# HGRN2 heads taken in pairs on tiles twice as wide, signed differences, a four-part output projection and another stream order in a two-layer hybrid trunk

## The chip, the core and the metric

The kernel runs on one core of a Trainium2 chip. The metric is device time in microseconds (us) of one execution. TensorE is called PE (PEld for its weight loads), VectorE DVE, ScalarE ACT, GpSimd POOL, and SyncE SP, whose queue issues the weight transfers.

## What is computed

A trunk of two layers on 256 tokens of 2048 features, all in float32. The change lies in layer 0, whose mixer joins two recurrences:

```python
q, f, i, g = split_cols(p_hg, HG_COLS)              # 8 heads of 128
k = (1.0 - lb) * jax.nn.sigmoid(-f)
q = jax.nn.silu(q)
o_hg = hgrn2_chunked(q, k, i, log_f)                # scores: q k exp(bcum[t] - bcum[s]), s <= t
o_hg = head_rmsnorm(unchunk_seq(o_hg), HG_HEADS, hg_norm) * jax.nn.sigmoid(g)
...
o_rw = rwkv7_scan(rh, decay, kh, vh, kk, a)         # 16 heads of 64
...
return jnp.concatenate([o_hg, o_rw], axis=-1) @ w_out
```

After each mixer comes a SwiGLU feed-forward of width 5632; layer 1 has an mLSTM and a Mamba2 mixer.

## The kernel before, in words

Every large product splits its float32 operands into a high and a low part: ACT rounds the weight tile `raw` into `whi`, DVE subtracts it into `wlo` (lines 262 and 263, seen at L262 and L109), and PE forms three products. A weight tile covers two blocks of 128 input rows; `raw`, `whi` and `wlo` have three buffers each, so ACT and DVE can be at most three tiles ahead of PE.

In layer 0 these products, the **bulk**, run beside two **lanes**, `rw` (RWKV7, four tasks of four heads, `rwkv_quad`, whose tiles are called `lane`) and `hg` (HGRN2, tiles with names that begin with h). All are Python generators that `flow` (lines 337 to 365) interleaves at build time: in each round both lanes take one step (a step that yields 1 rests one round), then the bulk takes three steps. The engines then run their own instructions in the order that is built; a list scheduler moves instructions of an engine a little within it. When the bulk reaches `wait` for a task that isn't done, it spends empty steps until the lane gets there.

The string `ORDER` sets the bulk: `p` is one pair of RWKV heads (`p0` to `p7`, products of 128x256, a task for every second one), `h` the next HGRN2 block: values and gates of four heads (`V0`, `V1`, products of 128x512), then queries and keys of two heads (`K0` to `K3`, 128x256). After `K` the HGRN2 work of its two heads is queued: a gates step `hgrn_gates` (Abs, Exp, Ln: two sets of activation tables), then `hgrn_head` for each. A head has a scan, the product qk, and for m = 1, 2, ..., 64 a function `decayed(m)`: difference, Abs, Exp, two products on DVE, then two matmuls and a copy_predicated into `hown`.

The output projection `out_proj` follows in three parts, called here Rw0 (512 rows, RWKV tasks 0 and 1), H (1024 rows, all of HGRN2) and Rw1 (512 rows, RWKV tasks 2 and 3); each ends a column block with two additions into the residual, and before Rw1 the bulk waits for RWKV task 3. The feed-forward begins behind Rw1.

Of the kernel before, what the change touches and what calls it, by code (L numbers as in the profile page):

```python
# [31 lines left out]


AHEAD = 2
ORDER = 'hhpphpphhpphpp'

EVEN_RATIO = 3.0
ODD_RATIO = 3.0
# [41 lines left out]
class Trunk:  # L80
    def __init__(self, ctx, tc, a, out):
        self.ctx, self.tc, self.nc, self.a, self.out = ctx, tc, tc.nc, a, out
        self.n = 0
        ep = lambda *x, **k: ctx.enter_context(tc.tile_pool(*x, **k))
        self.const = Arena(self.t(ep(name="const", bufs=1), [P, 1088], "const"))
# [59 lines left out]

    def masks(self):
        nc, c = self.nc, self.const
        self.rst2 = self.t(c, [P, 2, P], "rst2")
# [767 lines left out]
    def hgrn_head(self, hd, q, k, lf, vv, sg):
        nc, c, T = self.nc, self.c, self.T
        T2 = lambda tag: T(tag, (P, 2, P))
        ps2 = lambda: self.bank()[:, 0:S].rearrange("p (a t) -> p a t", t=P)
# [19 lines left out]
        own = T2("hown")  # L939
        ps = self.bank()[:, 0:8].rearrange("p (a n) -> p a n", n=4)  # L940
        for t in range(2):
            self.mm(ps[:, t, :], qk[:, t * P:(t + 1) * P], self.ones[:, 0:4])
        for t in range(2):
            self.ts(own[:, t, :], self.ident, ps[:, t, 0:1], ALU.mult)
        yield
        for m in (1, 2, 4, 8, 16, 32, 64):
            nh = P // (2 * m)
            ps = self.bank()[:, 0:P].rearrange("p (a j r) -> p a j r", a=2, r=m)
            for t in range(2):
                half = e.rearrange("p (j r) -> p j r", r=2 * m)[:, t * nh:(t + 1) * nh, m:2 * m]  # L950
                self.mm(ps[:, t], e[:, t * P:(t + 1) * P], half)
            mask = self.lev[m].bitcast(U32).rearrange("p (j r) -> p j r", r=2 * m)[:, :, m:2 * m]
            nc.vector.copy_predicated(out=own.rearrange("p a (j r) -> p a j r", r=2 * m)[:, :, :, m:2 * m],
                                      mask=mask.unsqueeze(1).broadcast_to([P, 2, nh, m]), data=ps)
            if m < 64:
                e = decayed(2 * m)
            else:

                e = T("he", bufs=3)
                self.ts(e[:, 0:P], b[:, 0:P], b[:, P - 1:P], ALU.subtract)  # L960
                self.act(e[:, 0:P], e[:, 0:P], AF.Exp, scale=-1.0)
                self.act(e[:, P:S], b[:, P:S], AF.Exp)
                self.mul(e[:, 0:P], e[:, 0:P], k[:, 0:P])
                self.mul(e[:, P:S], e[:, P:S], q[:, P:S])
# [6 lines left out]
        po = ps2()
        self.mm(po[:, 0, :], own[:, 0, :], vv[:, 0, :])
        self.mm(po[:, 1, :], cross, vv[:, 0, :], stop=False)
        self.mm(po[:, 1, :], own[:, 1, :], vv[:, 1, :], start=False)
        ss = T("hss", (P, 2))
        on = T2("hon")
        for t in range(2):
# [5 lines left out]
        for t in range(2):
            self.ts(on[:, t, :], on[:, t, :], ss[:, t:t + 1], ALU.mult)
        yield
        ps = self.bank()[:, 0:S]
        for t in range(2):
            self.tr(ps[:, t * P:(t + 1) * P], on[:, t, :])
        self.act(sg, ps.rearrange("p (t s) -> p t s", s=P), AF.Identity, scale=c["hg_norm"][:, hd:hd + 1])

# [29 lines left out]
    def gates(self, xt, bc, wk, rowp, cols):  # L1020
# [321 lines left out]
```

## Time and profile before

| | us |
|---|---|
| median of three runs | 2498.75 (2492.96 to 2506.86) |
| the profiled execution | 2492.96 |
| its span, first to last instruction | 2491.2 |
| PE busy in the span | 2446.7 |
| DVE busy | 1463.4 |
| ACT busy | 1137.6 |

The profiled execution is the fastest of the three runs; 1.8 us of it lie outside the span. In the time line, p0 begins at 124.82 us, Rw0 at 503.88, H at 535.90, Rw1 at 600.49, and the feed-forward of layer 0 at 636.33. A busy PE is not a PE at its peak, since matmuls overlap and a late one looks long.

### The profile page before, as it was taken

Reading aid. Unit: us, or ns where it says so; the run is one execution under the profiler, and the core shown is the slowest. Engines: PE = TensorE matmul, PEld = TensorE weight load, DVE = VectorE, ACT = ScalarE, POOL = GpSimd, SP = SyncE. Lnnn points to the kernel's source line nnn. Section 1 sums busy time; section 2 is a strip of 40 time slices with the busy share of each in tenths; the row PEclk is TensorE's granted clock in tenths of the full one; section 3 lists DMA queues with packets and bytes.
Section 4 is the critical chain, followed back from the end, with each engine's and each line's share of the span. In section 5 each row is a group of like instructions: output and inputs, shape, how many; then the busy total and the mean of one; then the engine's idle time right before and its main releaser. Section 6 shows DMA issues by size and latency. Waiting matters only on the chain.

```text
span 2491.2 us, 35908 instructions
## 1 busy us (share of the span) xinstructions
PE 2446.7 (98%) x14505; PEld 2078.1 (83%) x14505; DVE 1463.4 (59%) x2098; ACT 1137.6 (46%) x1499; POOL 43.3 (2%) x92
## 2 busy tenths in 40 slices
PE   7999999999999999999999999999999999999998
PEld 5899899977888888888888899888888888888886
DVE  3588768795644545445455778566645445454455
ACT  6465445542544444443444645453544344434443
POOL 2000000000000000000000000000000000000000
PEclk9999999999999999999999999999999999999999
DMA  5553445444555565555554554656555555555554
GB/s 152 169 150 100 139 115 145 136 132 160 180 189 186 187 200 188 186 188 200 186 186 152 152 165 144 182 174 228 169 190 195 190 189 188 195 188 191 195 188 136
DMA packets 271095, 428.79 MB, mean 172 GB/s; under 512 B 18363, under 2 KB 86193, under 8 KB 270801
## 3 DMA queue, kind: packets, MB, share of 16 engines
q1 hardware_dynamic: 270353, 425.45, 53.8%
q8 instruction: 114, 1.87, 0.3%
q10 hardware_dynamic: 576, 1.05, 0.1%
q14 instruction: 52, 0.43, 0.0%
HBM read 424.35 MB, written 2.10 MB: 171 GB/s over the span
## 4 chain that ended last, share of the span: by engine, by line
PE 92%; DVE 4%; ACT 1%; DMA 1%; issue 1%; POOL 0%; SPq 0%; POOLq 0%; ACTq 0%; DVEq 0%
PE b L130 84%; PE m L130 4%; PE m L606 3%; PE m L135 2%; DVE wlo L109 1%; DMA raw<-w_in_even 1%; ACT whi L262 0%; DMA act<-x 0%; ACT act L121 0%; DVE act L109 0%; DVE lane L103 0%; DMA raw<-w_in_odd 0%; ACT xs L121 0%; SPq L273 0%; DVE xs L103 0%
## 5 line engine op out<-in xcount | busy, mean ns | idle before, releaser
L130 PE MATMUL b<-whi,act 128*128 128x512 f32 x5376 | 1682.5, 392 | 6.6 <-ACT act L262 4.5
L109 DVE TENSOR_TENSOR wlo<-raw,whi 128x1024 fp32r<-128x1024 f32 (+2 forms) x818 | 978.5, 1198 | 877.2 <-ACT whi L262 876.0
L262 ACT CAST whi<-raw 128x1024 fp32r<-128x1024 f32 (+2 forms) x818 | 838.8, 1027 | 1165.1 <-PE b L130 1087.7
L130 PEld LDWEIGHTS b<-whi,act 128*128 128x128 f32 x5376 | 1010.2, 188 | 217.3 <-ACT act L262 4.8
L130 PE MATMUL b<-wlo,act 128*128 128x512 f32 x2688 | 1049.7, 391 | 0.4 <-DVE wlo L109 0.4
L130 PEld LDWEIGHTS b<-wlo,act 128*128 128x128 f32 x2688 | 505.6, 188 | 104.5 <-DVE wlo L109 1.4
L130 PE MATMUL b<-act,whi 128*128 128x256 f32 (+1 forms) x2048 | 387.0, 288 | 0.4 <-ACT act L262 0.2
L130 PEld LDWEIGHTS b<-act,whi 128*128 128x128 f32 (+1 forms) x2048 | 317.2, 190 | 4.0 <-issue 0.9
L130 PE MATMUL b<-act,wlo 128*128 128x256 f32 (+2 forms) x1024 | 290.5, 285 | 2.5 <-DVE wlo L109 2.3
L130 PEld LDWEIGHTS b<-act,wlo 128*128 128x128 f32 (+2 forms) x1024 | 193.7, 190 | 4.1 <-DVE wlo L109 3.8
L606 PEld LDWEIGHTS m<-lane 64*64 64x64 f32 x1920 | 67.9, 134 | 16.5 <-issue 7.2
L606 PE MATMUL m<-lane 64*64 64x64 f32 (+2 forms) x1920 | 79.3, 229 | 0.6 <-DVE lane L762 0.5
L106 DVE TENSOR_TENSOR act<-act,b 128x512 f32<-128x512 f32 x96 | 62.1, 681 | 11.5 <-PE b L130 11.4
L121 ACT ACTIVATE he<-he 128x256 f32<-128x256 f32 (+1 forms) x120 | 46.2, 406 | 19.1 <-DVE he L109 17.7
L121 ACT ACTIVATE sg<-b,rs 128x512 f32<-128x512 f32 x44 | 29.9, 688 | 19.9 <-PE b L130 19.9
L130 PE MATMUL m<-he 128*128 128x64 f32 (+1 forms) x240 | 36.7, 272 | 0.9 <-DVE he L103 0.9
L130 PEld LDWEIGHTS m<-he 128*128 128x128 f32 x240 | 32.7, 190 | 4.1 <-issue 1.3
L103 DVE TENSOR_TENSOR he<-he,act 128x128 f32<-128x128 f32 x128 | 31.8, 287 | 1.5 <-ACT he L121 1.5
L112 DVE SCALAR_TENSOR_TENSOR gu<-b,rs,sg 128x512 f32<-128x512 f32 x44 | 30.9, 743 | 0.0
L121 ACT ACTIVATE xs<-act 128x512 f32<-128x512 f32 x40 | 24.7, 620 | 11.9 <-DVE act L106 7.2
L109 DVE TENSOR_TENSOR act<-m,act 128x512 fp32r<-128x512 f32 x44 | 28.2, 683 | 0.0
L135 PE MATMUL m<-const,gu 128*128 128x128 f32 x176 | 27.6, 279 | 0.0
(238 smaller groups left out, 902.5 us busy)
## 6 DMA issues: line engine op xcount, KB each, us to landing
raw<-ffn_w_up SPq DMA_DIRECT2D x176, 1024.0 KB
raw<-ffn_w_down SPq DMA_DIRECT2D x88, 1024.0 KB
raw<-w_in_odd SPq DMA_DIRECT2D x88, 512.0 KB
raw<-w_in_even SPq DMA_DIRECT2D x192, 128.0 KB
raw<-w_in_even SPq DMA_DIRECT2D x32, 512.0 KB
raw<-w_in_even SPq DMA_DIRECT2D x64, 256.0 KB
raw<-w_out_even SPq DMA_DIRECT2D x32, 512.0 KB
raw<-w_out_odd SPq DMA_DIRECT2D x32, 512.0 KB
```

Source lines behind the costliest of these rows:

```text
L103: self.nc.vector.tensor_tensor(out=out, in0=a, in1=b, op=ALU.mult)
L106: self.nc.vector.tensor_tensor(out=out, in0=a, in1=b, op=ALU.add)
L109: self.nc.vector.tensor_tensor(out=out, in0=a, in1=b, op=ALU.subtract)
L112: self.nc.vector.scalar_tensor_tensor(out=out, in0=a, scalar=s, in1=b, op0=op0, op1=op1)
L121: self.nc.scalar.activation(out=out, in_=a, func=f, **k)
L130: self.nc.tensor.matmul(out, lhsT, rhs, start=start, stop=stop)
L135: self.nc.tensor.transpose(out=out, in_=in_, identity=self.ident[b:b + k, b:b + k])
L262: self.nc.scalar.copy(out=hi, in_=src)
L606: self.nc.tensor.matmul(out[s], lhsT[s], rhs[s], start=start, stop=stop)
```

## The change

Two heads become one task. `hgrn_heads` holds the gates step and both heads; its tiles are 128x512 (two heads of 256 tokens) where they were 128x256, so most instructions on DVE and ACT are half as many and twice as wide. The matmuls are as many as before. `decayed` writes differences with the sign that makes them negative, in two instructions on half the columns each, and the Abs on ACT goes. The squares of the norm are summed by a DVE reduction in place of accumulating activations. The output projection of HGRN2 is done in two parts of 512 rows. `ORDER` changes: K0 comes after p0 and p1, and K3 last of all, behind p7.

```diff
-ORDER = 'hhpphpphhpphpp'
+ORDER = 'hpphhpphpphpph'
...
         yield from rw(0)
-        yield from self.wait(*(f"hg{g}" for g in range(4)))
-        yield from self.out_proj(wo, lambda k: half(self.hgo[k // 4])[:, k % 4:k % 4 + 2], 0)
+        for i in range(2):
+            yield from self.wait(f"hg{i * 2}", f"hg{i * 2 + 1}")
+            yield from self.out_proj(wo, lambda k: half(self.hgo[i])[:, k:k + 2], i * 512, 4)
         yield from rw(1)
...
-        lf = T("hlf", (P, 2, S), 1)
-        self.put("hg", f"hg{g}", self.hgrn_gates(f, lf, lb, oml, g * 2))
-        for j in range(2):
-            sl = slice((g % 2 * 2 + j) * P, (g % 2 * 2 + j + 1) * P)
-            self.put("hg", f"hg{g}", self.hgrn_head(g * 2 + j, q[:, j, :], f[:, j, :], lf[:, j, :], self.vv[:, :, sl],
-                                                    self.hgo[g // 2][:, :, sl]))
+        sl = slice(g % 2 * S, (g % 2 + 1) * S)
+        self.put("hg", f"hg{g}", self.hgrn_heads(g * 2, q, f, self.vv[:, :, sl], self.hgo[g // 2][:, :, sl], lb, oml))
...
-        L, en = T("hL", (P, 2, S), 1), T("hen", (P, 2, S), 1)
+        L, en = (self.T("he", (P, 2, S), 3) for _ in range(2))
...
             e = T("he", bufs=3)
-            self.sub(V(e), V(b), V(b)[:, :, m - 1:m].broadcast_to([P, S // (2 * m), 2 * m]))
-            self.act(e, e, AF.Abs)
-            self.act(e, e, AF.Exp, scale=-1.0)
+            mid = V(b)[:, :, m - 1:m].broadcast_to([P, 2 * S // (2 * m), m])
+            self.sub(V(e)[:, :, 0:m], mid, V(b)[:, :, 0:m])
+            self.sub(V(e)[:, :, m:2 * m], V(b)[:, :, m:2 * m], mid)
+            self.act(e, e, AF.Exp)
             self.mul(V(e)[:, :, 0:m], V(e)[:, :, 0:m], V(k)[:, :, 0:m])
             self.mul(V(e)[:, :, m:2 * m], V(e)[:, :, m:2 * m], V(q)[:, :, m:2 * m])
...
-        for t in range(2):
-            self.act(T("hsq", (P, P)), po[:, t, :], AF.Square, accum_out=ss[:, t:t + 1])
+        self.act(sq, po, AF.Square)
+        nc.vector.tensor_reduce(out=ss, in_=sq.rearrange("p h t s -> p (h t) s"), axis=AX.X, op=ALU.add)
```

How the order of instructions moves, at three places. First ACT at the gates step of the first HGRN2 task (beside p0 before, beside K1 now); `act_617` holds q and f, and each ACT_TABLE_LOAD changes the set of functions. Before:

```order
L121 ACTIVATE hL_1188<-act_617 128x512
L121 ACTIVATE hL_1188<-hL_1188 128x512
L121 ACTIVATE hen_1189<-hen_1189 128x512
L121 ACT_TABLE_LOAD
L121 ACTIVATE hL_1188<-hL_1188 128x512
L121 ACTIVATE hen_1189<-hen_1189,masks_105_593 128x256 x2
L262 CAST whi_1278<-raw_1277 128x2x384
L121 ACT_TABLE_LOAD
L121 ACTIVATE act_617<-act_617 128x512
```

Now:

```order
L121 ACTIVATE he_1732<-act_617 128x512
L121 ACTIVATE he_1732<-he_1732 128x512
L121 ACT_TABLE_LOAD
L121 ACTIVATE he_1732<-he_1732 128x512
L121 ACT_TABLE_LOAD
L121 ACTIVATE he_1733<-he_1733 128x512
L754 COPY lane_606<-m_1785 128x2x192
L121 ACT_TABLE_LOAD
L121 ACTIVATE he_1733<-he_1733,masks_105_593 128x256 x2
L121 ACT_TABLE_LOAD
L121 ACTIVATE act_617<-act_617 128x512
```

The second Exp has moved behind the first Ln, so there are four table loads where there were two, and no weight cast stands among them; the second task has four as well, the third and fourth two.

Second, DVE in Rw0: what stands ahead of one weight subtraction `wlo`. Before (the piece is the end of 20 rows between two `wlo`):

```order
L109 TENSOR_TENSOR he_6130<-hb_5910 128x256
L109 TENSOR_TENSOR lane_606<-m_5997,lane_606 128x512
L953 COPY_PREDICATED hown_5979<-masks_249,m_6082 128x64x2
L112 SCALAR_TENSOR_TENSOR rkv_5197<-b_5673,const_58,rkv_5197 128x255
L953 COPY_PREDICATED hown_5979<-masks_249,m_6126 128x32x4
L833 TENSOR_REDUCE lane_606<-lane_606 128x8
L112 SCALAR_TENSOR_TENSOR rkv_5197<-b_5673,const_58,rkv_5197 128x255
L118 TENSOR_SCALAR lane_606<-lane_606 128x8
L112 SCALAR_TENSOR_TENSOR rkv_5197<-b_5674,const_58,rkv_5197 128x255
L109 TENSOR_TENSOR act_6107<-act_295,act_6107 128x512 x2
L103 TENSOR_TENSOR he_6130<-he_6130,act_617 128x16x8 x2
L109 TENSOR_TENSOR wlo_6144<-raw_6142,whi_6143 128x1024
```

Now (the end of 19 rows between two `wlo`):

```order
L106 TENSOR_TENSOR hlf_5769<-hlf_5769,he_5771 128x512
L103 TENSOR_TENSOR lane_606<-m_5830,masks_105_593 128x256
L924 SCALAR_TENSOR_TENSOR hb_5811<-const_58,hlf_5769 128x512
L118 TENSOR_SCALAR act_617<-act_617,masks_105_593 128x256 x2
L103 TENSOR_TENSOR lane_606<-m_5860,masks_105_593 128x4x2x64
L103 TENSOR_TENSOR he_5813<-act_617 128x512
L109 TENSOR_TENSOR he_5815<-hb_5811 128x256 x2
L103 TENSOR_TENSOR lane_606<-m_5870,masks_105_593 128x4x2x64
L733 TENSOR_REDUCE lane_606<-lane_606 128x64
L103 TENSOR_TENSOR he_5815<-he_5815,act_617 128x256 x2
L103 TENSOR_TENSOR hown_5881<-const_58,m_5882 128x512
L109 TENSOR_TENSOR wlo_5893<-raw_5891,whi_5892 128x1024
```

The gates and the first level of the last HGRN2 task now meet the middle of the last RWKV task, ahead of one weight subtraction.

Third, PE at the end of the last RWKV task, whose turned output is `m<-const,lane`. Before, what follows it are products of Rw1 (`act_7113`) that need its result:

```order
L130 MATMUL b_7159<-whi_7161,act_7113 128x512
L130 MATMUL m_7092<-const_58,lane_606 64x64 x16
L130 MATMUL b_7118<-whi_7139,act_7113 128x512
L130 MATMUL b_7118<-wlo_7140,act_7113 128x512
L130 MATMUL b_7118<-whi_7139,act_7113 128x512
```

Now products of the second HGRN2 part (`act_6510`) follow, which don't:

```order
L130 MATMUL b_6665<-whi_6685,act_6510 128x512
L130 MATMUL m_6696<-const_58,lane_606 64x64 x16
L130 MATMUL b_6664<-whi_6685,act_6510 128x512
L130 MATMUL b_6664<-wlo_6686,act_6510 128x512
L130 MATMUL b_6664<-whi_6685,act_6510 128x512
```

## Rows read from the trace of the kernel before

**Rows 1.** The page: busy time by engine, and the chain that ended last.
```profile
PE 2446.7 (98%) x14505; PEld 2078.1 (83%) x14505; DVE 1463.4 (59%) x2098; ACT 1137.6 (46%) x1499; POOL 43.3 (2%) x92
...
PE 92%; DVE 4%; ACT 1%; DMA 1%; issue 1%; POOL 0%; SPq 0%; POOLq 0%; ACTq 0%; DVEq 0%
```

**Rows 2.** Windows of layer 0's mixer: stretch, busy us (and instructions) by engine, clock, DMA.
```profile
80.02:101.78 21.76, 21.76 (x97) 18.02 (x96) 9.80 (x8) 9.49 (x11) 0.00 (x0) 1.00 0.67 195
101.78:124.82 23.04, 23.04 (x194) 23.03 (x193) 10.12 (x10) 9.08 (x11) 0.00 (x0) 1.00 0.57 161
124.82:148.44 23.62, 21.35 (x175) 20.56 (x174) 18.85 (x46) 19.22 (x36) 0.00 (x0) 1.00 0.45 119
148.44:169.03 20.59, 20.59 (x176) 20.50 (x175) 16.28 (x40) 12.37 (x26) 0.85 (x1) 1.00 0.70 197
326.40:359.00 32.60, 32.60 (x402) 30.45 (x400) 16.61 (x29) 10.46 (x14) 0.00 (x0) 1.00 0.40 111
567.90:585.05 17.15, 17.15 (x194) 13.12 (x192) 10.30 (x17) 5.45 (x7) 0.00 (x0) 1.00 0.41 127
503.88:535.90 32.02, 30.39 (x200) 24.35 (x201) 30.05 (x64) 18.56 (x33) 5.16 (x3) 1.00 0.36 116
600.49:636.33 35.84, 31.54 (x253) 26.07 (x249) 23.16 (x33) 11.18 (x13) 1.64 (x1) 0.90 0.59 195
124.82:636.33 511.51, 499.38 (x5091) 446.41 (x5089) 395.22 (x894) 249.42 (x440) 21.16 (x16) 0.99 0.47 136
```

**Rows 3.** Time line of PE, then ACT, at Rw1: start, us, instruction, idle before it.
```profile
608.99 0.39 PE L130 MATMUL b<-whi,act 128*128 128x512 f32 x1
610.30 1.15 PE L130 MATMUL m<-const,lane 64*64 64x64 f32 x32 [0.92 <-DVE lane L103]
614.83 0.79 PE L130 MATMUL b<-whi,act 128*128 128x512 f32 x1 [3.38 <-ACT act L262]
...
619.68 0.75 PE L130 MATMUL b<-whi,act 128*128 128x512 f32 x2
...
614.16 0.62 ACT L262 CAST act<-act 128x512 fp32r<-128x512 f32 x1 [3.65 <-DVE act L103]
```

**Rows 4.** Groups by form, DVE, 124.82 to 636.33: count, busy us, mean ns, idle before.
```profile
L103 DVE TENSOR_TENSOR he<-he,act 128x128 f32<-128x128 f32 x128 | 31.8, 287 | 1.5 <-ACT he L121 1.5
L109 DVE TENSOR_TENSOR he<-hb 128x256 f32<-128x256 f32 x56 | 22.9, 420 | 0.0
L953 DVE COPY_PREDICATED hown<-masks,m 128x128 f32<-128x128 uint32 x56 | 19.0, 340 | 8.3 <-PE m L130 7.6
L106 DVE TENSOR_TENSOR act<-act,b 128x512 f32<-128x512 f32 x24 | 16.0, 684 | 6.3 <-PE b L130 6.3
...
L922 DVE TENSOR_TENSOR_SCAN hb<-const,hlf 128x256 f32<-128x256 f32 x8 | 5.5, 684 | 0.0
...
L670 DVE TENSOR_TENSOR_SCAN lane<-masks,act 128x512 f32<-128x512 f32 x3 | 3.7, 1218 | 0.0
```

**Rows 5.** The same groups of ACT.
```profile
L121 ACT ACTIVATE he<-he 128x256 f32<-128x256 f32 x112 | 44.2, 414 | 19.0 <-DVE he L109 17.7
...
L121 ACT ACT_TABLE_LOAD x8 | 10.3, 1283 | 0.1
L121 ACT ACTIVATE lane<-lane 128x512 f32<-128x512 f32 x11 | 6.9, 625 | 7.4 <-DVE lane L109 5.9 <-DVE lane L116 1.0 <-PE m L130 0.5
```

**Rows 6.** Time line at the first gates step, beside p0: ACT, then DVE, then PE.
```profile
126.25 0.63 ACT L121 ACTIVATE hL<-act 128x512 f32<-128x512 f32 x1
...
128.08 1.28 ACT L121 ACT_TABLE_LOAD   x1
129.37 0.63 ACT L121 ACTIVATE hL<-hL 128x512 f32<-128x512 f32 x1
...
134.64 0.39 DVE L103 TENSOR_TENSOR he<-act 128x256 f32<-128x256 f32 x1
134.96 0.41 DVE L109 TENSOR_TENSOR he<-hb 128x256 f32<-128x256 f32 x1
...
135.18 0.58 PE L130 MATMUL m<-const,he 128*128 128x4 f32 x4 [0.75 <-DVE he L103]
```

More of the change, by code (lines that the diff above doesn't have):

```diff
@@ L84, in __init__ @@
         ep = lambda *x, **k: ctx.enter_context(tc.tile_pool(*x, **k))
-        self.const = Arena(self.t(ep(name="const", bufs=1), [P, 1088], "const"))
+        self.const = Arena(self.t(ep(name="const", bufs=1), [P, 1344], "const"))
         self.act_pool = ep(name="act", bufs=10)
@@ L147, in masks @@
         nc, c = self.nc, self.const
-        self.rst2 = self.t(c, [P, 2, P], "rst2")
+        self.rst2 = self.t(c, [P, 4, P], "rst2")
         nc.gpsimd.memset(self.rst2, 1.0)
@@ L913, in hgrn_gates, with hgrn_heads @@
             self.ts(k[:, j, :], k[:, j, :], oml[:, hd + j:hd + j + 1], ALU.mult, 0.5, ALU.mult)
+    def hgrn_heads(self, hd, q, k, vv, sg, lb, oml):
+        nc, c = self.nc, self.c
+        W = (P, 2, S)
+        T = lambda tag, shape=W, bufs=1: self.T(tag, shape, bufs)
+        flat = lambda x: x.rearrange("p h s -> p (h s)")
+        quarters = lambda x: x.rearrange("p (a t) -> p a t", t=P)
+        heads = lambda x: x.rearrange("p t (h s) -> p h t s", s=P)
+        lf = T("hlf")
+        self.hgrn_gates(k, lf, lb, oml, hd)
         yield
[L916 to L919, printed above, removed]
         b = T("hb")
-        nc.vector.tensor_tensor_scan(out=b, data0=self.rst2.rearrange("p c t -> p (c t)"), data1=lf, initial=0.0,
-                                     op0=ALU.mult, op1=ALU.add)
+        nc.vector.tensor_tensor_scan(out=flat(b), data0=self.rst2.rearrange("p c t -> p (c t)"), data1=flat(lf),
+                                     initial=0.0, op0=ALU.mult, op1=ALU.add)
         qk = T("he", bufs=3)
@@ L927, in decayed @@
         def decayed(m):
-            V = lambda x: x.rearrange("p (j r) -> p j r", r=2 * m)
+            V = lambda x: flat(x).rearrange("p (j r) -> p j r", r=2 * m)
             e = T("he", bufs=3)
-            self.sub(V(e), V(b), V(b)[:, :, m - 1:m].broadcast_to([P, S // (2 * m), 2 * m]))
-            self.act(e, e, AF.Abs)
-            self.act(e, e, AF.Exp, scale=-1.0)
+            mid = V(b)[:, :, m - 1:m].broadcast_to([P, 2 * S // (2 * m), m])
+            self.sub(V(e)[:, :, 0:m], mid, V(b)[:, :, 0:m])
+            self.sub(V(e)[:, :, m:2 * m], V(b)[:, :, m:2 * m], mid)
+            self.act(e, e, AF.Exp)
             self.mul(V(e)[:, :, 0:m], V(e)[:, :, 0:m], V(k)[:, :, 0:m])
@@ L938, in hgrn_head @@
         yield 1
-        own = T2("hown")
-        ps = self.bank()[:, 0:8].rearrange("p (a n) -> p a n", n=4)
-        for t in range(2):
-            self.mm(ps[:, t, :], qk[:, t * P:(t + 1) * P], self.ones[:, 0:4])
-        for t in range(2):
-            self.ts(own[:, t, :], self.ident, ps[:, t, 0:1], ALU.mult)
+        own = T("hown", (P, 4, P))
+        ps = self.bank()[:, 0:16].rearrange("p (a n) -> p a n", n=4)
+        for a in range(4):
+            self.mm(ps[:, a, :], quarters(flat(qk))[:, a, :], self.ones[:, 0:4])
+        self.mul(own, self.ident.unsqueeze(1).broadcast_to([P, 4, P]), ps[:, :, 0:1].broadcast_to([P, 4, P]))
         yield
@@ L947, in hgrn_head @@
             nh = P // (2 * m)
[L948 to L951, printed above, removed]
+            ps = self.bank()[:, 0:S].rearrange("p (a j r) -> p a j r", a=4, r=m)
+            ef = flat(e)
+            for a in range(4):
+                half = ef.rearrange("p (j r) -> p j r", r=2 * m)[:, a * nh:(a + 1) * nh, m:2 * m]
+                self.mm(ps[:, a], ef[:, a * P:(a + 1) * P], half)
             mask = self.lev[m].bitcast(U32).rearrange("p (j r) -> p j r", r=2 * m)[:, :, m:2 * m]
             nc.vector.copy_predicated(out=own.rearrange("p a (j r) -> p a j r", r=2 * m)[:, :, :, m:2 * m],
-                                      mask=mask.unsqueeze(1).broadcast_to([P, 2, nh, m]), data=ps)
+                                      mask=mask.unsqueeze(1).broadcast_to([P, 4, nh, m]), data=ps)
             if m < 64:
@@ L959, in hgrn_head @@
                 e = T("he", bufs=3)
[L960 to L964, printed above, removed]
+                lo, hi = slice(0, P), slice(P, S)
+                self.sub(e[:, :, lo], b[:, :, P - 1:P].broadcast_to([P, 2, P]), b[:, :, lo])
@@ L965, in hgrn_head @@
+                self.act(e[:, :, hi], b[:, :, hi], AF.Exp)
+                self.act(e[:, :, lo], e[:, :, lo], AF.Exp)
+                self.mul(e[:, :, hi], e[:, :, hi], q[:, :, hi])
+                self.mul(e[:, :, lo], e[:, :, lo], k[:, :, lo])
             yield
-        ps = self.bank()[:, 0:P]
-        self.mm(ps, e[:, 0:P], e[:, P:S])
-        cross = T("hcr", (P, P))
+        ps = self.bank()[:, 0:S].rearrange("p (h t) -> p h t", t=P)
+        for h in range(2):
+            self.mm(ps[:, h, :], e[:, h, 0:P], e[:, h, P:S])
@@ L969, in hgrn_head @@
+        cross = T("hcr", (P, 2, P))
         nc.scalar.copy(out=cross, in_=ps)
         yield
[L971 to L977, printed above, removed]
-            self.act(T("hsq", (P, P)), po[:, t, :], AF.Square, accum_out=ss[:, t:t + 1])
-        for t in range(2):
-            self.mul(on[:, t, :], po[:, t, :], sg[:, t, :])
+        po = self.bank().rearrange("p (h t s) -> p h t s", h=2, t=2)
@@ new lines, in hgrn_heads @@
+        for h in range(2):
+            v = vv[:, :, h * P:(h + 1) * P]
+            self.mm(po[:, h, 0, :], own[:, h * 2, :], v[:, 0, :])
+            self.mm(po[:, h, 1, :], cross[:, h, :], v[:, 0, :], stop=False)
+            self.mm(po[:, h, 1, :], own[:, h * 2 + 1, :], v[:, 1, :], start=False)
+        ss = T("hss", (P, 4))
+        sq, on = (T("he", (P, 2, 2, P), 3) for _ in range(2))
+        self.act(sq, po, AF.Square)
+        nc.vector.tensor_reduce(out=ss, in_=sq.rearrange("p h t s -> p (h t) s"), axis=AX.X, op=ALU.add)
@@ L981, in hgrn_head @@
         self.rsqrt(ss, 1.0 / P, EPS)
+        self.mul(on, po, heads(sg))
+        yield 1
+        on4 = on.rearrange("p h t s -> p (h t) s")
+        self.mul(on4, on4, ss.unsqueeze(2).broadcast_to([P, 4, P]))
         yield
[L983 to L989, printed above, removed]
+        ps = self.bank().rearrange("p (h t s) -> p h t s", h=2, t=2)
@@ L993, in gate_consts @@
+        for h in range(2):
+            for t in range(2):
+                self.tr(ps[:, h, t, :], on[:, h, t, :])
+            self.act(heads(sg)[:, h], ps[:, h], AF.Identity, scale=c["hg_norm"][:, hd + h:hd + h + 1])
     def gate_consts(self):
@@ L1062, in gates @@
         self.stt(sp, x, 0.0, q, ALU.max, ALU.add)
-        rst = self.rst2.rearrange("p c t -> p (c t)")
+        rst = self.rst2[:, 0:2].rearrange("p c t -> p (c t)")
         colp = self.t(wk, [P, S], "colp")
```

1 line of the change is left out of this document (removed).

## The prediction

> **What bounds the kernel now.** I read the page first: PE is busy for 2446.7 of 2491.2 us, DVE for 59%, ACT for 46%, and the chain that ended last lies on PE for 92% [rows 1]. So work taken off DVE or ACT counts only where PE waits for it. The feed-forward blocks and layer 1 hold nothing that the diff touches but the slice of `rst2`; what can move lies between p0 and the feed-forward of layer 0, 511.51 us [rows 2].
>
> How much of that is not PE's own work? Two windows without a lane give the pace of the bulk: 96 matmuls of 128x512 in 21.76 us, 0.227 each, and 192 of 128x256 in 23.04, 0.12 each [rows 2]. The windows behind p0 with one lane give the lanes' price. p1 takes 20.59 us, of which its 144 bulk matmuls are 17.28: 3.31 for 30 records of hg, 0.11 each. K2 takes 32.60, 23.04 of them bulk: 9.56 for 208 records of rw, 0.046; the third column block of H 17.15, with 48 bulk matmuls at 0.227 (10.90): 6.25 for 144, 0.043 [rows 2]. I take 0.044. From p0 on the bulk is 8 pairs at 17.28, 3 key blocks at 23.04, 2 blocks V1 at 21.8 and 384 output matmuls at 0.227, together 338; hg's 352 records are 38.7, rw's 2312 are 101.7, and some 120 others, put at 0.08 (between both), 9.7. Of 511.5 us 488 are PE's own, so **23.4 us is excess**, 0.94% of the kernel. No relief of DVE or ACT can give more.
>
> Where does it lie? Rw1 has the most: 35.84 us, clock 0.90. p0 has 23.62 − 17.28 − 28 × 0.11 = 3.3, Rw0 about 2.6; p1 has none [rows 2]. The rest is spread in pieces of at most 1.7.
>
> **The change, part by part.** *The wait before Rw1* is one place. PE gets the last RWKV task's output transposes at 610.30 after 0.92 us without work, then stands 3.38 us until ACT's cast at 614.16 has made its operand: 4.3 us. From 614.83 on it works at the lower clock (1.2 instead of 2.4 GHz): eleven matmuls stand between that row and the one at 619.68, 4.85 us where 11 × 0.227 = 2.50, so 2.35 more [rows 3]. In the new order the work after these transposes is the second HGRN2 part (third excerpt), and a whole part of 96 matmuls (21.8 us) precedes Rw1. Both go: **−6.7 us**. What is late next is nothing that I find, since Rw1's operands are then long there; if the gap returned at the HGRN2 part, this term would be 0. K3 comes last, so its task finishes nearer to its use, but Rw0 and the first HGRN2 part (43.6 us of bulk) stand ahead of that.
>
> *Fewer, wider instructions.* DVE's 128 products of 128x128 (31.8 us) become 64 of 128x256 at about 0.41 (26.5), its 56 copy_predicated of 128x128 (19.0) 28 of twice the size, by the same slope 0.47 each (13.2), eight scans of 0.684 four of 1.218; the differences stay 56 of 128x256; eight more additions into the residual cost 8 × 0.684 [rows 4]. Sum −5.3 − 5.8 − 0.6 + 5.5 = −6 us of DVE's 395 in this stretch. On ACT 112 activations of 0.414 (44.2) become 28 of 0.63, about 17.6, and four table loads of 1.283 come on top: −26.6 + 5.1 = −21 of 249 [rows 5]. Neither engine has the longer sum here (DVE 395, ACT 249, PE 499 [rows 2]), and PE's matmuls are as many. So the work is hidden under PE and the term is **0**; if PE were waiting for DVE throughout, it would be −6. The rows speak for a small saving: a tile twice as wide takes 684 ns for 420, only 156 less than two [rows 4].
>
> A rule of the Trainium skill bears on this (*VectorE: DVE Perf Modes*, "The TRN2 errata"): operations on SBUF pay a fixed latency per instruction, so tiles of 512 and more are advised. By its formula for fp32, (N+151)/0.96 ns, some 140 fewer instructions would take 22 us off DVE, an estimate. The rows show the same fixed part, but instructions that start before the last one ends: 128 of 287 ns were 31.8 us, not 36.7 [rows 4]. That is the page's side of the first rival.
>
> *The gates step.* Beside p0 it ran from Abs at 126.25 to the first difference at 134.96, 8.7 us, with two table loads; PE got its first HGRN2 matmul at 135.18 and had waited [rows 6]. In the new order the first two tasks have four loads each, and scan and product are wider: 8.7 + 2 × 1.28 + 0.53 + 0.3 = 12.1. A load costs its 1.28 and hardly more: the one at 128.08 is followed by the ACTIVATE at 129.37 [rows 6]. The bulk in front of the first HGRN2 matmul is 69 matmuls where it was 68, so the first task pays the longer chain nearly whole (+3.4). The second has 60 in its own block and 63 more, by the order, before it, and the last two keep two loads. RWKV work, which p0 had not, covers a little more in K1. I take **+3.5**; bounds −3.3 (p0's excess goes) and +6.8 (both tasks pay in full).
>
> The Trainium skill speaks against this edit (*ScalarE: Activation LUTs*, "What ACT_TABLE_LOAD costs"): every switch of sets costs 1283 ns and a drain of about 1380, 2.66 us. The row agrees on the load and shows no such drain, 0.01 us to the next ACTIVATE. By the page the four extra loads would be 10.6 us, by the rows 5.1.
>
> *The lanes pressed together.* p0 and p1 lose their HGRN2 work, which comes back in K1, p2, p3, p6 and Rw0. Rw0 is the place to watch: it took 32.02 us with DVE busy for 30.05 and PE for 30.39 [rows 2]. Summed over the order with durations of rows 4, DVE has 39 us of instructions between the first and the last matmul of Rw0 before and 48 now, PE 29 and 37 with its lanes. The longest run of DVE work ahead of one `wlo` there (second excerpt) grows from 9.0 to 13.9 us, where two tiles of bulk and their lane work cover about 8.3; in p3 one grows to 9.8 over a cover of 6.1. Queued behind each is a `wlo`, for which PE waits. If all of it showed it were 5.6 + 3.7 = +9; but Rw0 stood at nearly 9 over its cover before and lost only 2.6. I take **+3**, bounds 0 and +9.
>
> *p0 and p1 without a lane.* PE then eats the weights faster: 8 tiles of 393 KB in 17.28 us, 182 GB/s. V0g moved 195 and p1 itself 197 without an idle PE [rows 2]. **0**; the bound above is +3.3, the excess of p0, if the stream can't hold it.
>
> *Four parts instead of three.* The additions are counted above, the splits of the operands once for each tile as before. **0.**
>
> Sum: −6.7 + 0 + 3.5 + 3 + 0 + 0 = −0.2 us. The profiled execution's 2492.96 (its span and 1.8 around it) becomes 2492.8. It is the fastest of its three; against the median, 5.8 above it, I forecast **2498.5**. A measurement of this kernel tells about 0.5%, 12.5 us, from no change.
>
> **The rivals.** *Faster: the relief reaches PE.* If the scattered excess comes from DVE's and ACT's many small instructions that stand in front of `wlo` and `whi`, halving them gives back most of it. For it speaks that DVE takes 30.05 of 32.02 us in Rw0 [rows 2]; against it that p1 has no excess with its lane running, and V0g none. Of the 23.4 the 6.7 at Rw1 go, and of the other 16.7 some 10 to 12: −17 to −19, about 2481. Chance 0.18.
>
> *Slower: DVE's run in front of one `wlo` empties the pipe.* PE can be three tiles ahead at most; where the gates and the first levels of a task meet the middle of an RWKV task, PE stands until the run is through. It decides when the run passes the cover of two tiles, as it does by my sums in K1, p3 and Rw0. The price is the excess run, 9 in all, the longer gates of two tasks, 6.8, and after each stall of some 3 us the lower clock, 2.35 as at Rw1 [rows 3], three times; less the 6.7: 9 + 6.8 + 7 − 6.7 = +16, about 2515. Against it: before, Rw0's gaps didn't lower the clock (1.00 [rows 2]). Chance 0.18.
>
> *The wait at Rw1 stays*, or moves to the second HGRN2 part because the interleaving leaves the RWKV task as late as it was: +6.5, about 2505, still within 0.5%. Chance 0.1; the order speaks against it, as 96 matmuls that need none of it lie between.
>
> **How the numbers follow.** My forecast has 0.54: within 2492 and 2507 by its bounds that are likeliest. With the third rival it makes "within 0.5%" 0.64; 0.18 to either side. The range of 2483 to 2513 reaches nearly to both rivals' times and leaves out about one in ten on each side.
>
> **What would show it.** Right: no wait of PE for `act` at Rw1 and a clock of 1.00 there; the stretch from p0's place to the feed-forward as long as before within 6 us, counted from the first matmul after V0; in DVE's groups 64 products of 128x256 where there were 128, and ACT below 235 us; waits of PE for `he` at K1 of 4 us or more; twelve table loads. Wrong: windows of K1, p2 and Rw0 that equal their own work (then the relief was real), or a clock under 1.00 in Rw0 or K1 (then the second rival). If the lone p0 and p1 take more than 18 us each, the stream was my error.

## The result, and the profile after

| | before | after |
|---|---|---|
| median of nine runs, us | 2504.68 (2492.75 to 2507.11) | 2515.57 (2512.28 to 2529.58) |
| ratio, 95% interval | | 1.0070 (1.0044 to 1.0096) |
| span of the profiled execution | 2491.2 | 2522.4 |
| V0's first matmul to V0's gate half | 38.81 | 51.18 |
| V0's gate half to the feed-forward of layer 0 | 556.31 | 576.15 |

The change makes the kernel 0.7% slower. In some executions of nearly every kernel here (by their times, five of the nine of before and three of the nine of after) the V0 block itself runs at the lower clock, 12.4 us longer (the fourth line of the table); the profile of after is one of these and that of before is not, so I compare the **stretch** from V0's gate half to the feed-forward, in which the change lies: **+19.8 us**. The lowest of the nine runs, 2492.75 and 2512.28, lie 19.5 us apart, which agrees with it; the medians are only 10.9 us apart. Behind the stretch nothing moved (1854.87 us to the end before, 1854.47 after).

The page of after: busy time by engine, and the chain that ended last.

```profile
PE 2473.4 (98%) x14505; PEld 2096.2 (83%) x14505; DVE 1460.1 (58%) x1966; ACT 1115.8 (44%) x1379; POOL 45.2 (2%) x88
...
PE 92%; DVE 3%; ACT 2%; DMA 1%; issue 1%; POOL 0%; SPq 0%; POOLq 0%; ACTq 0%; DVEq 0%
```

Against [rows 1] DVE and ACT do less and PE is busy for longer, with as many matmuls: at the lower clock a matmul takes longer (32 small ones 1.55 us instead of 1.12, below). Where this happened the windows show (V0, then the stretch, p1, K1, p3, p6, Rw0, Rw1; columns as in [rows 2]):

```profile
40.60:91.78 51.18, 49.90 (x162) 30.41 (x161) 17.85 (x39) 24.76 (x46) 0.00 (x0) 0.73 0.31 92
91.78:667.93 576.15, 558.80 (x5378) 501.74 (x5376) 411.64 (x780) 245.67 (x340) 22.37 (x12) 0.97 0.46 134
130.81:148.09 17.28, 17.28 (x146) 17.28 (x145) 9.56 (x12) 8.20 (x12) 0.00 (x0) 1.00 0.73 198
179.04:229.27 50.23, 45.51 (x531) 43.66 (x529) 36.02 (x94) 26.36 (x38) 0.00 (x0) 0.90 0.20 56
261.93:294.89 32.96, 29.80 (x244) 28.94 (x243) 25.93 (x53) 15.30 (x25) 3.67 (x2) 0.90 0.37 104
433.84:478.06 44.22, 43.05 (x458) 40.77 (x457) 30.80 (x84) 19.59 (x32) 0.00 (x0) 0.77 0.20 53
537.21:580.90 43.69, 39.43 (x363) 31.93 (x362) 39.89 (x99) 22.28 (x34) 0.00 (x0) 1.00 0.25 80
643.42:667.93 24.51, 24.51 (x122) 20.47 (x120) 17.01 (x21) 10.40 (x11) 0.00 (x0) 1.00 0.88 295
```

And the same stretch before:

```profile
80.02:636.33 556.31, 544.18 (x5378) 487.46 (x5376) 415.15 (x912) 267.99 (x460) 21.16 (x16) 0.99 0.48 139
```

Two columns give the sum. Span less PE busy is the time in which PE stood: 12.1 us before, 17.4 after. Length times what is missing of the clock is an estimate of what the lower clock took: 3.6 us at Rw1 before [rows 2], now 50.23 × 0.10 + 32.96 × 0.10 + 44.22 × 0.23 = 18.5 in K1, p3 and p6. The two parts are +5.2 and +14.9, together 20.1, where 19.8 were measured. **Three quarters of the loss is PE's clock; the waits that it falls behind are short.** Two windows inside K1 and p6 show the lower clock by itself:

```profile
194.40:204.64 10.24, 10.24 (x88) 9.89 (x85) 4.75 (x10) 1.42 (x2) 0.00 (x0) 0.50 0.18 53
446.99:467.47 20.48, 20.18 (x167) 19.09 (x163) 12.65 (x29) 3.75 (x7) 0.00 (x0) 0.50 0.16 39
```

PE's waits in the stretch (us in total, times, longest):

```profile
PE m L607 <- DVE lane L763: 6.0, 2, 4.7
PE m L130 <- DVE he L103: 4.1, 4, 1.9
PE b L130 <- DVE wlo L109: 3.8, 3, 1.7
PE m L135 <- ACT act L121: 2.1, 1, 2.1
```

They are waits for results of the lanes (`lane`, `he`) more than for weights (`wlo`). The longest stands at the first gates step, in K1. The time line of ACT, then DVE, then PE, and PE in p6 just before its clock falls:

```profile
182.00 1.28 ACT L121 ACT_TABLE_LOAD   x1
183.29 0.63 ACT L121 ACTIVATE he<-he 128x512 f32<-128x512 f32 x1
183.94 1.28 ACT L121 ACT_TABLE_LOAD   x1
...
186.24 1.28 ACT L121 ACT_TABLE_LOAD   x1
...
188.47 1.28 ACT L121 ACT_TABLE_LOAD   x1
189.76 0.63 ACT L121 ACTIVATE act<-act 128x512 f32<-128x512 f32 x1
190.30 0.46 ACT L754 COPY lane<-m 128x384 f32<-128x384 f32 x1
...
190.95 1.22 DVE L924 TENSOR_TENSOR_SCAN hb<-const,hlf 128x512 f32<-128x512 f32 x1
...
193.34 0.44 DVE L763 STREAM_TRANSPOSE lane<-lane 128x256 f32<-128x256 f32 x1
...
193.92 1.55 PE L607 MATMUL m<-lane 64*64 64x32 f32 x32 [4.72 <-DVE lane L763]
...
441.78 1.12 PE L607 MATMUL m<-lane 64*64 64x32 f32 x32
...
445.76 0.47 PE L130 MATMUL m<-const,he 128*128 128x4 f32 x3 [0.87 <-DVE he L103]
```

The RWKV lane's STREAM_TRANSPOSE on DVE stands behind the scan and the first differences of HGRN2, and these behind four table loads. PE, in order, waits 4.72 us for it, and then 32 small matmuls take 1.55 us (the same number took 1.12 in p6 before its clock fell).

### The profile page after: what moved, and what is told of

The parts are those of the page before. It is cut to its first block, busy times and chain, and to the rows that moved or that the text cites. A ratio compares the mean times of both kernels' runs of the same rounds, so it can differ in the third digit from the quotient of the medians.

```text
span 2522.4 us, 35592 instructions
## 1 busy us (share of the span) xinstructions
PE 2473.4 (98%) x14505; PEld 2096.2 (83%) x14505; DVE 1460.1 (58%) x1966; ACT 1115.8 (44%) x1379; POOL 45.2 (2%) x88
## 4 chain that ended last, share of the span: by engine, by line
PE 92%; DVE 3%; ACT 2%; DMA 1%; issue 1%; POOL 0%; SPq 0%; POOLq 0%; ACTq 0%; DVEq 0%
PE b L130 83%; PE m L130 4%; PE m L607 3%; PE m L135 1%; DVE wlo L109 1%; DMA raw<-w_in_even 1%; ACT whi L262 0%; ACT L121 0%; ACT he L121 0%; DMA act<-x 0%; DMA raw<-w_in_odd 0%; DVE act L106 0%; ACT act L121 0%; DMA raw<-w_out_even 0%; ACT xs L121 0%
## 5 line engine op out<-in xcount | busy, mean ns | idle before, releaser
L130 PEld LDWEIGHTS b<-act,whi 128*128 128x128 f32 (+1 forms) x2048 | 322.8, 193 | 6.3 <-issue 2.3
L106 DVE TENSOR_TENSOR act<-act,b 128x512 f32<-128x512 f32 x104 | 67.3, 680 | 7.2 <-PE b L130 7.1
L121 ACT ACTIVATE he<-he 128x512 f32<-128x512 f32 (+1 forms) x44 | 26.3, 609 | 34.4 <-DVE he L109 34.2
L121 ACT ACTIVATE sg<-b,rs 128x512 f32<-128x512 f32 x44 | 29.9, 688 | 19.9 <-PE b L130 19.8
L121 ACT ACT_TABLE_LOAD x24 | 30.8, 1283 | 3.2 <-PE b L130 2.1
```

Source lines behind the costliest of these rows:

```text
L106: self.nc.vector.tensor_tensor(out=out, in0=a, in1=b, op=ALU.add)
L121: self.nc.scalar.activation(out=out, in_=a, func=f, **k)
L130: self.nc.tensor.matmul(out, lhsT, rhs, start=start, stop=stop)
```

## The experiments

For each kernel the stretch is given (one profiled execution) and the ratio to the kernel before. Most blocks that two kernels share agree within 0.1 us, but not all: Rw0 is 43.69 us long in after and, with the same three waits (1.9, 1.2 and 1.1 us), 48.28 in two_loads and fill, where the clock fell. So differences of less than some 5 us need the times of all runs beside them. Rw0 in fill:

```profile
513.12:561.40 48.28, 44.04 (x362) 35.95 (x361) 40.11 (x98) 22.28 (x34) 0.00 (x0) 0.89 0.23 73
```

**Order against tiles.** Three kernels take the change apart.

```diff
# old_order: the changed kernel with
-ORDER = 'hpphhpphpphpph'
+ORDER = 'hhpphpphhpphpp'
# four_parts: the kernel before with
-        yield from self.wait(*(f"hg{g}" for g in range(4)))
-        yield from self.out_proj(wo, lambda k: half(self.hgo[k // 4])[:, k % 4:k % 4 + 2], 0)
+        for i in range(2):
+            yield from self.wait(f"hg{i * 2}", f"hg{i * 2 + 1}")
+            yield from self.out_proj(wo, lambda k: half(self.hgo[i])[:, k:k + 2], i * 512, 4)
# order_parts: four_parts and the new ORDER
```

> The changed kernel with the old ORDER string; wide tiles, signed differences and the four-part projection stay. I read the stretch from the first matmul of V0's gate half to the feed-forward of layer 0: 556.3 us before, 576.2 after. Theory 1 (the new order does the harm: it puts gates and heads where the RWKV lane is dense, PE waits there and its clock falls): about 546 to 552 us, two table loads at the first gates step, no lower clock inside the stretch, the kernel faster than before by 4 to 10 us. Theory 2 (the wide tiles do it: longer instructions ahead of wlo and of the RWKV lane, in any order): 565 us or more, with the clock falling in the blocks that carry HGRN2.

> The kernel before, its heads one by one with Abs and 128x256 tiles, with the new ORDER and the four-part projection. Theory 1 (the order does the harm): the stretch from V0's gate half to the feed-forward takes 570 us or more, four table loads at the first gates step, waits and a lower clock in K1 and p6. Theory 2 (the wide tiles do it): about 550 us, the 556.3 of before less the 6.7 of the tail.

> The kernel before with the four-part output projection alone. Both theories, and the term of the prediction: the wait before Rw1 and the lower clock there go, the stretch from V0's gate half to the feed-forward is 556.3 - 6.7 = 549.6 us. Rival: the wait moves to the second HGRN2 part, or the extra additions cost as much: 554 to 557 us.

| stretch, us (95% interval of the ratio) | one head a task | two heads a task |
|---|---|---|
| old order, four parts | 558.4 (0.9984 to 1.0023) | 594.0 (1.0175 to 1.0210) |
| new order, four parts | 554.4 (0.9961 to 1.0003) | 576.2 (1.0044 to 1.0096) |

Theory 1, mine, fell. The new order gains in both columns (4.0 and 17.8 us; the medians of four_parts and order_parts, 2494.36 and 2489.13, agree with the first); two heads in a task lose in both rows (35.6 and 21.8). The right column has all that came with the pairs, the signed differences and the norm's reduction too. Nor do four parts alone remove the wait before Rw1: in the window of Rw1 in four_parts PE stands for 4.30 us, as before; with the new ORDER it goes, since RWKV's last task is through earlier (its transposes start 8.0 us before Rw1 in after, 9.8 us behind its start in before). In order_parts a shorter wait, 1.7 us for the operand of the last HGRN2 task, stands in the second HGRN2 part instead, and the clock falls behind it. Rw1 in four_parts, then the second HGRN2 part in order_parts:

```profile
602.36:637.33 34.97, 30.67 (x252) 25.43 (x249) 23.16 (x33) 11.18 (x13) 1.64 (x1) 0.95 0.60 200
575.58:609.14 33.56, 31.63 (x252) 25.89 (x252) 25.16 (x51) 13.29 (x25) 2.33 (x2) 0.95 0.54 180
```

In old_order the loss is in p0, p2, p4 and p6 (three of them here), and PE waits for `he`:

```profile
123.90:156.94 33.04, 28.39 (x202) 27.47 (x201) 23.75 (x51) 17.84 (x27) 0.00 (x0) 0.85 0.28 75
374.12:415.07 40.95, 34.26 (x346) 32.59 (x345) 28.91 (x63) 18.33 (x28) 1.74 (x1) 0.87 0.22 57
468.81:512.93 44.12, 43.06 (x458) 40.79 (x457) 30.82 (x77) 19.59 (x32) 0.00 (x0) 0.77 0.21 53
```

```profile
PE m L130 <- DVE he L103: 12.3, 10, 2.5
```

No engine is full there: in p4 DVE is busy for 28.91 of 40.95 us.

**The gates step.** two_loads takes the clamp of f at −80 out, so that the second Exp needs no DVE first and the scheduler leaves it beside the first. parts_two does the same to order_parts.

```diff
-        self.ts(en, f, -80.0, ALU.max)
-        self.act(en, en, AF.Exp, scale=-1.0)
+        self.act(en, f, AF.Exp, scale=-1.0)
```

> The changed kernel without the clamp of f at -80 ahead of the second Exp, so that both Exps stand together on ACT and the gates step has two or three table loads instead of four; the output is the same as long as no f lies below -80. Theory 1a (the long gates chain starts it: the wait of 4.72 us at K1 brings the lower clock of 10.24 us): the wait falls to about 2, and if that is short enough the clock holds: the stretch is 566 to 571 us instead of 576.2. Theory 1b (the clock falls for the sparse work of two lanes, whatever the wait): only the 2.6 us of the wait go, twice at the most: 571 to 574, and the clock falls at the same places.

> The kernel of order_parts (one head at a time, new ORDER, four parts; stretch 554.4 us) with the clamp at -80 left out of the gates step, so that the Exps stand together and two table loads go. The long gates chain is what PE waits for in K1 (2.69 us, then 6.83 us at the lower clock): both should go, 547 to 551 us, and the kernel is 0.2 to 0.4% under the kernel before. Rival: the wait at K1 is for the RWKV lane behind the first head's own work and stays: 553 to 556.

two_loads: 567.1, −9.0 (ratio 1.0068, 1.0046 to 1.0091). Each of the first two tasks has two loads less. K1 falls from 50.23 to 41.87 us at full clock; its two loads are 2.6 us of that. In Rw0 the lower clock took back some 5 us of the gain. parts_two, with two loads less in all: 546.6, −7.8 against order_parts, and no lower clock in the stretch (ratio **0.9954**, 0.9939 to 0.9969: the best of all). K1 in two_loads, then the stretch and K1 in parts_two:

```profile
179.18:221.05 41.87, 41.42 (x530) 39.40 (x529) 35.37 (x92) 23.73 (x36) 0.00 (x0) 1.00 0.24 68
```

```profile
78.99:625.58 546.59, 541.82 (x5377) 485.44 (x5376) 416.94 (x916) 271.20 (x462) 22.01 (x16) 1.00 0.49 141
166.24:203.12 36.88, 36.88 (x494) 35.21 (x493) 30.99 (x89) 23.87 (x43) 0.00 (x0) 1.00 0.35 98
```

**Does the wait lower the clock?** fill gives PE idle work ahead of the wait in K1 and in p6.

```diff
+        self.xh0 = xt(0)[0]
...
         e = decayed(1)
+        if hd in (0, 4):
+            fill = self.bank()[:, 0:S]
+            for _ in range(36):
+                self.mm(fill, self.xh0[:, 0:P], self.xh0)
```

> The changed kernel with 36 idle matmuls of 128x256 (about 4.3 us, their result is not read) behind the first difference of the first and the third HGRN2 task, ahead of the bulk of that round: work added in K1 and p6. Theory 1a (the wait lowers the clock): in K1 they fill the wait of 4.72 us, the clock holds there, the block K1 (50.2 us) takes about 45; in p6 there is a wait of 0.87 only, they cost up to 4.3, and the clock of p6 tells whether that wait or the sparse work behind it lowers it: if it holds, p6 (44.2) takes 36 to 39. Theory 1b (sparse work, not the wait, lowers the clock): both blocks keep their lower clock; K1 the same 50, p6 up to 48.

The stretch with some 8.6 us of useless matmuls more is 568.7, **7.4 us shorter** than without (ratio 1.0035, 1.0012 to 1.0058; after 1.0070). K1 and p6 hold the clock, p6 even where only a wait of 0.87 us was, and are 9.0 us shorter together; Rw0, where the clock fell, is 4.6 us longer:

```profile
166.91:212.96 46.05, 45.28 (x567) 43.57 (x565) 37.89 (x98) 26.09 (x38) 0.00 (x0) 1.00 0.28 76
417.64:457.09 39.45, 39.45 (x518) 37.78 (x517) 33.92 (x92) 22.11 (x37) 0.00 (x0) 1.00 0.28 72
```

The added matmuls fill the wait and also make PE's work denser, so fill alone does not tell these two apart. The traces of all 15 kernels help: 47 times the clock falls in V0 or in the stretch, and each time during a wait of PE of 0.5 us or more or just behind one. The reverse does not hold: waits as long pass without it, as those in Rw0 of after do. So a wait stands at every fall here, and what else decides stays open.

**Rounds or wide instructions?** In the kernel before, two heads take some 30 rounds one after the other; a task of two takes 16, with the same levels. narrow_pair runs two tasks of one head at once, with no wide instruction. spread, old_spread and even_two (with spread_two between) stretch the wide task over more rounds: the step that yields 1 or 2 rests that many rounds.

```diff
# narrow_pair, on the kernel before
-            self.flow(self.even_bulk(xt, w), dict(rw=1, hg=1), EVEN_RATIO)
+            self.flow(self.even_bulk(xt, w), dict(rw=1, hg=2), EVEN_RATIO)
# spread on the changed kernel, old_spread on old_order, spread_two on two_loads: at the end of a level
-            yield
+            yield 1
# even_two, on spread_two
-            yield 1
+            yield 2
```

> The kernel before with one number changed: the flow keeps two HGRN2 tasks of one head going at once (hg=2 in place of hg=1); tiles, instructions, ORDER and the three-part projection stay. Theory 3 (what hurts is that two heads' levels fall in the same rounds, so that the same chain has half the bulk to lie beside): the stretch from V0's gate half to the feed-forward, 556.3 us before, goes to 570 or more, with waits for he and a lower clock in p0, p2, p4 and p6, as in old_order (594.0). Rival 4 (the wide instructions hurt): none are there, so 553 to 559.

> The run old_order (wide tiles, old ORDER, stretch 594.0 us) with the seven levels resting one round each, as in the run spread. Theory 3: the waits for he (15 us) and the lower clock (54 us of it inside the stretch) of p0, p2, p4 and p6 go for the most part: 556 to 568. Rival 4: 588 or more.

> The changed kernel with one line different: each of the seven levels of an HGRN2 task rests one round (yield 1 in place of yield), so six bulk steps instead of three stand between the matmuls of two levels. Theory 3 (a task of two heads has a level's difference, Exp, two products and copy for both heads in one round, so the same chain has half the bulk to lie beside; PE waits for he, and its clock falls): the waits for he and the lower clock at p3 and p6 shrink, the stretch from V0's gate half to the feed-forward falls from 576.2 to 555 to 566 us; the wait of 4.72 at the first gates step and its lower clock stay. Rival 4 (the wide instructions themselves cost: a longer DVE or ACT instruction ahead of wlo and of the RWKV lane, wherever it stands): no change, 573 to 579.

> The resting levels of the run spread together with the gates step of the run two_loads (no clamp at -80, two table loads). Theory 3: the two gains add, the 9.0 us that two_loads took off the stretch (567.1) and what spread takes off: 546 to 557 us; if it comes under 554.4 (order_parts: one head at a time in the new order) the wide tiles are no loss in themselves, and the whole beats the kernel before by up to 0.4%. Rival 4: 565 or more.

> The kernel of spread_two (wide tiles, new ORDER, four parts, two table loads; stretch 556.8 us) with two resting rounds a level in place of one: a task of two heads then takes some 30 rounds, as two tasks of one head do in parts_two (stretch 546.6). Theory 3 in full (only the rounds count): 545 to 550 us. Rival 4 for the rest (a wide instruction in the way costs something of its own: in Rw0, p3 and p6 a wlo or the RWKV lane stands behind twice the work at once): 553 to 559 us, with waits for wlo and lane left in these places.

narrow_pair: 581.1, +24.8 on the kernel before, without one wide instruction (ratio 1.0111, 1.0088 to 1.0134). PE's waits for `he` and for `wlo` are 8.6 us each, and the clock falls in p0, p4 and p6, not in p2. Its stretch, then p4 and p6:

```profile
78.77:659.89 581.12, 555.28 (x5377) 496.93 (x5376) 417.38 (x912) 268.45 (x460) 22.67 (x16) 0.98 0.46 133
367.66:400.85 33.19, 29.17 (x330) 28.06 (x329) 25.73 (x66) 21.07 (x40) 1.64 (x1) 0.95 0.31 83
458.91:496.97 38.06, 36.31 (x438) 35.01 (x437) 29.90 (x86) 22.98 (x46) 0.00 (x0) 0.87 0.29 74
```

old_spread: 564.2 (ratio 1.0034, 1.0009 to 1.0059), 29.8 of the 35.6 us back by one resting round a level. In the old order theory 3 holds for the most part.

spread: 574.3, only −1.9 and short of what I expected (ratio 1.0052, 1.0038 to 1.0067). The ten runs say more than this one execution of 2510.05 us: they go down to 2504.80, 7.5 us below the lowest of after, which is still short. p6 falls to 38.85, but the first task ends later, and the second one's gates step then meets p3, where PE waits 6.8 us at once for `he`:

```profile
246.16:278.59 32.43, 24.96 (x214) 24.45 (x213) 25.83 (x50) 21.26 (x31) 2.66 (x2) 0.89 0.39 103
```

spread_two, with the short gates step: 556.8, −10.3 against two_loads (ratio 1.0007, 0.9981 to 1.0033).

even_two, with as many rounds as one head at a time: 558.6, not better (ratio 1.0044, 1.0016 to 1.0072), against 546.6 of parts_two. So **12 us of the loss are not the rounds**, and theory 3 does not hold in full: of the 20.5 us between two_loads and parts_two the resting rounds give back 8.6. (The profiled execution of even_two is the fastest of its eight runs, 2493.53 to 2515.65, so 12 is the least.) PE stands for 11.7 us in even_two's stretch and 4.8 in that of parts_two; the other 5 us are about what the lower clock takes in its stretch (0.99, against 1.00).

```profile
78.79:637.35 558.56, 546.82 (x5378) 489.61 (x5376) 410.98 (x776) 239.95 (x336) 20.62 (x12) 0.99 0.48 139
```

The second column block of Rw0 shows some of the 12, even_two first, then parts_two:

```profile
509.85:524.57 14.72, 12.83 (x113) 10.72 (x111) 14.43 (x37) 5.88 (x9) 0.00 (x0) 0.88 0.11 37
```

```profile
503.56:514.22 10.66, 10.59 (x115) 8.71 (x113) 10.66 (x31) 6.32 (x10) 0.00 (x0) 1.00 0.07 20
```

In even_two the scan and the first level of both heads stand in one step: DVE is busy nearly throughout, 3.8 us longer than in parts_two, and PE waits for it. The block is 4.1 us longer, but Rw0 as a whole is 2.1 us shorter, as lane work moves on into the HGRN2 parts. By blocks the 12 us are K1 (+1.7), V1 (+5.4), p6 (+1.9), p3 (−1.0) and all from K3 to Rw1 (+4.4). I did not split these further. parts_two also lacks the signed differences and the norm's reduction, so that the 12 us are the task of two heads as it is written and need not all be the width of its instructions.

**Signed differences alone**, on one head at a time, order_parts with

```diff
-            self.sub(V(e), V(b), V(b)[:, :, m - 1:m].broadcast_to([P, S // (2 * m), 2 * m]))
-            self.act(e, e, AF.Abs)
-            self.act(e, e, AF.Exp, scale=-1.0)
+            mid = V(b)[:, :, m - 1:m].broadcast_to([P, S // (2 * m), m])
+            self.sub(V(e)[:, :, 0:m], mid, V(b)[:, :, 0:m])
+            self.sub(V(e)[:, :, m:2 * m], V(b)[:, :, m:2 * m], mid)
+            self.act(e, e, AF.Exp)
```

> The kernel of order_parts (one head at a time, new ORDER, four parts; stretch 554.4 us) with the signed differences alone: two subtractions on 128 of the 256 columns each, no Abs on ACT. DVE then has 56 instructions of 0.287 us more than before less 56 x (0.420 - 0.287), ACT 56 of 0.414 less. Theory 3 (a level's chain is what PE waits for): the chain is shorter by some 0.3 us a level, 551 to 555 us. Rival 4 (DVE's busy time is what counts): 8 us more on DVE, 556 to 560.

557.7 against 554.4 (ratio 0.9991, 0.9973 to 1.0009, where order_parts has 0.9982): no gain, and in the range of rival 4; a difference of 3.3 us alone would prove little, but the medians, 2489.13 and 2493.39, go the same way. ACT's 20.6 us less in the stretch bring nothing.

**The V0 block.** parts_two_fill adds idle work ahead of the wait in V0 (1.26 us in before, 1.28 in after), on parts_two, in `lora`:

```diff
+            if p == 0:
+                fill = self.bank()[:, 0:S]
+                for _ in range(20):
+                    self.mm(fill, wa[0:64, cs], tl[0:64])
             self.mm(pg, g2[:, cs], gl, stop=False)
```

> The kernel of parts_two with 20 idle matmuls of 64x128x256 (some 3.5 us, their result is not read) ahead of the first of the low-rank products in the V0 block, where PE waits 1.2 to 1.3 us in every run and in some runs then goes at the lower clock for 27.3 us (the profiled execution of after had that, the one of before not). Theory (that wait sets the low clock): no run of this kernel shows it; its runs lie within 0.3% of each other, where those of the other kernels fall in two groups some 12 us apart; the fastest ones are up to 3 us slower than those of parts_two. Rival: the two groups stay.

Ten runs lie within 2488.77 and 2491.57 us, where before, beside it, had 14 between 2491.3 and 2495.3 and four between 2504.2 and 2510.3. The filling costs more than thought: V0 takes 45.76 us where parts_two took 38.87, so the four runs of parts_two (2481.63 to 2482.66) stay the fastest of all (ratio of parts_two_fill 0.9978, 0.9964 to 0.9992). By their times V0 did not slow down in any of those four either, so it is not shown that the filling is what kept it from that.

## Why the prediction was wrong

I forecast a change of −0.2 us, 2498.5, within 0.5%; the kernel became 0.7% slower, outside my range, and the stretch 19.8 us longer.

- *What bounds the kernel.* Right: PE. But I read the excess of 23.4 us only as the most that could be gained. It was no bound on a loss, and I had no row for what a loss would cost. The 23.4 itself, a difference of estimates, was too much: PE stood for 12.1 us of the stretch and the lower clock took 3.6.
- *Fewer, wider instructions: the step that failed.* The sizes were near: 64 products of 0.418 (predicted 0.41), 28 copies of 0.524 (0.47), twelve table loads; DVE 3.5 us less in the stretch where I had 6, ACT 22.3 less where I had 21. What failed is "the work is hidden under PE and the term is 0", which compared sums over 511 us. A lane is beside PE for a number of rounds, and the change halves these: a level of both heads, a chain of difference, Exp, products and copy, then has three bulk steps to lie beside where it had six. PE then waits for the lane's result and goes on at the lower clock. The term was +21.8 us in the new order and +35.6 in the old. narrow_pair shows the mechanism without wide tiles, and old_spread takes most of it back in the old order. In the new order the rounds are the smaller part: even_two leaves 12 us that belong to the wide task as it is written, and their cause stays open.
- *The lower clock* I priced in the second rival alone, at 2.35 us a stall. It took 10.2 us in p6 behind a wait of 0.87, which that price could not foresee. With idle work there (fill) the clock holds.
- *The gates step.* The mechanism was right (four loads, a chain of 12 us with PE waiting), the size not: +3.5 predicted; undoing the four extra loads, two in each of the first two tasks, gives 9.0 us, with the 5.0 us of clock in K1. The wait in K1 was 4.72 us, as my sign asked, but for `lane` and not for `he`: the RWKV lane's transpose stood on DVE behind the gates' results. The Trainium skill, *ScalarE: Activation LUTs*, "What ACT_TABLE_LOAD costs", counts a drain on top of each load. The trace agrees on 1283 ns and again shows no drain (183.29 + 0.63 to the next load at 183.94).
- *The lanes pressed together.* +3, bounds 0 to 9. By the table the order as a whole, with the wait at Rw1 and the gates step in it, is a gain, −4.0 with one head a task; I had read its crowding as the danger. What I saw in Rw0 is there, 4.3 us without PE, but the clock held; in two_loads and fill it did not.
- *The wait at Rw1.* Right for this kernel: no wait, 24.51 us, clock 1.00. It needs the order; the four parts alone don't do it, and with one head a task another wait, 1.7 us for the last HGRN2 task (K3 comes last), stands in the second HGRN2 part.
- *p0 and p1 without a lane.* Right: 17.28 us for p1.
- *The rivals.* The second one's time, 2515, was the measured 2515.57, partly by chance: it was +16 on a median of three runs that nine put 5.9 us higher, where the stretch has +19.8; its waits were to be for `wlo`, which are 3.8 us of 17, and its third stall was to be in Rw0, not p6. That PE is emptied where the gates meet the RWKV lane and then goes on at the lower clock was right, and so was my sign of it, a clock under 1.00 in K1. I gave it 0.18.

## What to carry to other kernels

Where side work is interleaved with a bound engine by rounds, count its chain per round against the work that the bound engine has in a round: halving the instructions by halving the rounds can starve the bound engine, though no other engine's total is full. Read the granted clock of each window before trusting "98% busy", and price a wait of TensorE with what its clock does afterwards. A single dependent instruction (here a clamp on another engine) can change how a scheduler groups activation functions; taking it out of the unchanged heads, with the new order and the four parts, was worth 0.5%. (Without it the output is the same only as long as no f lies below −80.)

## What was not expected of the hardware

After waits of 0.87 to 4.72 us PE went on at 1.2 GHz and lost 3 to 10 us in a block of after: about as much as it had stood in K1 and p3, and 10.2 us behind a wait of 0.87 in p6; adding useless matmuls ahead of the wait made the block faster (K1 50.23 to 46.05, p6 44.22 to 39.45). The same wait does not always do it. Rw0 has the same waits in after, two_loads and fill, and the clock held in after alone. In V0 PE waited about 1.3 us in before and in after, and only the latter then took 25.13 us for 60 matmuls that took 14.53:

```profile
46.58 14.53 PE L130 MATMUL m<-lora,act 128*128 128x256 f32 x60 [1.26 <-ACT lora L121]
```

```profile
45.97 25.13 PE L130 MATMUL m<-lora,act 128*128 128x256 f32 x60 [1.28 <-ACT lora L121]
```
